# Spreading SSD decay sums and norm factors over the partitions by DMA through DRAM in place of matmuls

## The chip, the cores and the metric

The kernel runs on one core of one Trainium2 chip. The metric is the device time of one execution in microseconds; before the change it is 1229.57 us, the median of three runs (1229.18 to 1230.66). A core has five engines, each with its own queue of instructions that it takes strictly in order: TensorE (PE; its weight loads are listed as PEld), VectorE (DVE), ScalarE (ACT), GpSimd (POOL) and SyncE (SP, which here only issues DMAs). They meet through semaphores. DMA transfers are issued from an engine's queue and carried out by the core's 16 DMA engines.

## The reference, cut to what matters

The program is one layer of a hybrid model on 512 tokens of 1024 values: a norm and an input projection, a state-space branch (SSD), a windowed attention branch, a merge, and a mixture of 64 experts. The change touches two places of the SSD branch: the decay matrix, which needs the running sum `a_cum` of each head along the tokens as rows and as columns, and the group norm at its end.

```
a_cum = jnp.cumsum(dt_c * a.reshape(G, J), axis=2)
seg = a_cum[:, :, :, None] - a_cum[:, :, None, :]
decay = jnp.exp(jnp.where(causal, seg, -jnp.inf)).astype(xs.dtype)
cb = jnp.einsum('bclgn,bcsgn->bclsg', cm, bm)
y_diag = jnp.einsum('bclsgj,bcsgjp->bclgjp', cb[..., None] * decay, xdt)
...
y_off = jnp.einsum('bclgn,bcgjpn->bclgjp', cm, prev) * jnp.exp(a_cum)[..., None].astype(xs.dtype)
y = (y_diag + y_off + xs * d_skip.reshape(G, J)[:, :, None].astype(xs.dtype)).reshape(b, s, SSD_D_INNER)
yz = (y * jax.nn.silu(z)).reshape(b, s, G, SSD_D_INNER // G)
return rms_norm(yz, ssd_norm_g.reshape(G, -1)).reshape(b, s, SSD_D_INNER)
```

There are 32 heads in 4 groups, and 4 chunks of 128 tokens. `rms_norm` takes one factor for each token and group.

## The kernel before

**Stages.** The work goes in two parts. The first, up to about 745 us, makes the projections, the two branches and the merge. Nearly all of its matmuls are projections: `proj` loads 1 MB of weights into one of two buffers `w`, splits each half into a high and a low part (`split`: ScalarE line 181, VectorE or GpSimd line 182, four buffers `g`) and multiplies 512 columns three times per 128 rows (lines 196 to 198). The second part streams 192 expert matrices of 1 MB through a ring of 14 buffers (`ra`, `rb`, line 779) and multiplies them (lines 904 and 925).

**What sets the order.** The code is written stage by stage (`xbc_stage`, `ssd_main`, `z_stage`, `ssd_norm`, `gate_stage`, the attention stages), and the framework's scheduler interleaves the stages on each engine at build time by its own estimate. After that each engine's order is fixed, and an instruction whose inputs are late holds up all that stands behind it on its engine. This holds for SyncE's queue too, which issues all weight loads.

**The decay sums.** `dt_stage` forms `acum` (128 tokens of a chunk on the partitions, 4 chunks times 32 heads as columns), transposes it, and keeps it as a high and a low half in `aT`, heads on the partitions. For each of the 32 heads, `decay` in `ssd_main` spreads the head's row of 512 sums over all 128 partitions by one matmul with a column of `sel` (line 365, into a PSUM tile `sb`). From it ScalarE takes an exponential (line 368, tile `E`), VectorE a minimum with the column sums (line 369, tile `M`), ScalarE four exponentials in place (line 374), VectorE or GpSimd a product with `cbm` (line 386), and PE multiplies (lines 382 and 390 in `heads`). `heads` ends with lines 392 and 394 on VectorE, which empty the two PSUM tiles `y`.

**The norm.** `ssd_norm` runs once for each of the four groups. PE sums the squares (line 406), VectorE scales (line 408), GpSimd takes the power -0.5 (line 409). The factors then lie on the partitions, by token, and are wanted along the columns: VectorE puts them on a diagonal (line 412, four instructions), PE multiplies by ones (line 414), and VectorE applies them from PSUM (line 418, four instructions). Lines 420 and 421 split the result for the next projection.

Small tiles of all these steps come from a pool `v` of 10 buffers of 512 columns, given out in turn.

Of the kernel before, what the change touches and what calls it, by code (L numbers as in the profile page):

```python
# [7 lines left out]
F = mybir.dt.float32  # L8
R = mybir.dt.float32r
# [3 lines left out]
AF = mybir.ActivationFunctionType  # L13
OP = mybir.AluOpType
# [16 lines left out]
def tile_hybrid(ctx: ExitStack, tc: tile.TileContext, x, pos, cols, rows, g2d, wrd, wdtd, wcm, wqkv, wso, wao, wo,  # L31
                wgu, wdn, out):
    nc = tc.nc
    V, S, T, G = nc.vector, nc.scalar, nc.tensor, nc.gpsimd
# [4 lines left out]
    def ptile(tag, bufs=2, dt=F):  # L39
        return psum.tile([128, 512], dt, name=tag, tag=tag, bufs=bufs)  # L40
# [26 lines left out]
    V.memset(half, 0.5)  # L67
    sel = pb.tile([128, 32], R, name="sel")
    G.memset(sel.bitcast(F), 0.0)
    V.tensor_tensor(sel[0:64], ident[0:64, 0:32], ident[0:64, 32:64], op=OP.add)  # L70
    colt = pb.tile([128, 168], F, name="colt")
# [45 lines left out]
    gwd = dram.tile([1024, 1], F, name="gwd")  # L117
    gtd = dram.tile([2, 8, 128, 512], F, name="gtd")

    def wslot(pool, tag, bufs, dt=F):  # L120
# [18 lines left out]
    def g_(): return tk(pg, "g", 4, 1024, R)  # L139
    def v_(dt=F, n=512): return pv.tile([128, n], dt, name="v", tag="v", bufs=10, padded_shape=[128, 512])  # L140
    def c_(dt=F, n=512): return pc.tile([128, n], dt, name="c", tag="c", bufs=6, padded_shape=[128, 512])
# [64 lines left out]
    nacum = pb.tile([128, 128], F, name="nacum")  # L206
    aT = pb.tile([128, 512], R, name="aT")
    G.memset(aT[64:128].bitcast(F), 0.0)

    def dt_stage():  # L210
# [6 lines left out]
        p = ptile("mm")  # L217
# [44 lines left out]
        S.activation(dec, dec, AF.Exp)  # L262
        a2 = v_(n=256)
        a2v = a2.rearrange("p (t u h) -> p t u h", t=4, u=2)
        for u in range(2):
            V.tensor_copy(a2v[:, :, u, :], acum.rearrange("p (t h) -> p t h", t=4))
        pt = ptile("tp")
        for t in range(4):
            T.transpose(pt[0:64, t * 128:(t + 1) * 128], a2[:, t * 64:(t + 1) * 64], ident)
        S.activation(aT[0:32], pt[0:32], AF.Copy)  # L270
        hv = v_(R)
        S.activation(hv[32:64], pt[32:64], AF.Copy)
        V.tensor_tensor(aT[32:64], pt[32:64], hv[32:64].bitcast(F), op=OP.subtract)

# [47 lines left out]
    def ssd_main(g):  # L322
# [37 lines left out]
        def decay(i, u):  # L360
            h = 8 * g + 2 * i + u
            if u == 0:
                Es[i] = v_()
            pb_ = ptile("sb")
            T.matmul(pb_, sel[:, h:h + 1].to_broadcast([128, 128]), aT, start=True, stop=True)
            M = v_()
            us = slice(u * 64, (u + 1) * 64)
            S.activation(Es[i][us, 0:384], pb_[us, 128:512], AF.Exp)
            V.tensor_tensor(M.rearrange("p (c l) -> p c l", c=4), pb_.rearrange("p (c l) -> p c l", c=4),
                            acum.rearrange("p (c h) -> p c h", c=4)[:, :, h:h + 1].to_broadcast([128, 4, 128]),  # L370
                            op=OP.min)
            for c in range(4):
                s = slice(c * 128, (c + 1) * 128)
                S.activation(M[:, s], M[:, s], AF.Exp, bias=nacum[:, c * 32 + h:c * 32 + h + 1])
            return M

# [26 lines left out]
    def ssd_norm(g):  # L403
# [5 lines left out]
        G.tensor_tensor(rs, rs, mhalf.to_broadcast([128, 4]), op=OP.pow)  # L409
        dg = v_()  # L410
        for t in range(4):
            V.tensor_scalar(dg[:, t * 128:(t + 1) * 128], ident, rs[:, t:t + 1], None, op0=OP.mult)
        pr = ptile("sb")
        T.matmul(pr, ones, dg, start=True, stop=True)
        for i in range(4):
# [871 lines left out]
```

## Time and profile before

| | |
|---|---|
| median of three runs | 1229.57 us |
| the profiled execution | 1228.64 us |
| its span in the trace | 1226.8 us |
| PE busy | 1136.3 us, 93% |
| VectorE busy | 656.5 us, 54% |
| ScalarE busy | 388.6 us, 32% |
| GpSimd busy | 239.3 us, 20% |
| bytes moved by DMA | 273.86 MB |

The span is the part of the execution between the first and the last instruction of the trace; the remaining 1.8 us lie around it. Engine times are sums of instruction durations. PE's instructions overlap (the next begins before the last has ended), so what one PE instruction costs is read from the distance between starts, not from its duration. Idle time of an engine that nobody waits for costs nothing.

### The profile page before, as it was taken

Reading aid. Unit: us, or ns where it says so; the run is one execution under the profiler, and the core shown is the slowest. Engines: PE = TensorE matmul, PEld = TensorE weight load, DVE = VectorE, ACT = ScalarE, POOL = GpSimd, SP = SyncE. Lnnn points to the kernel's source line nnn. Section 1 sums busy time; section 2 is a strip of 40 time slices with the busy share of each in tenths; the row PEclk is TensorE's granted clock in tenths of the full one; section 3 lists DMA queues with packets and bytes.
Section 4 is the critical chain, followed back from the end, with each engine's and each line's share of the span. In section 5 each row is a group of like instructions: output and inputs, shape, how many; then the busy total and the mean of one; then the engine's idle time right before and its main releaser. Section 6 shows DMA issues by size and latency. Waiting matters only on the chain.

```text
span 1226.8 us, 16583 instructions
## 1 busy us (share of the span) xinstructions
PE 1136.3 (93%) x6552; PEld 772.2 (63%) x6552; DVE 656.5 (54%) x1224; ACT 388.6 (32%) x796; POOL 239.3 (20%) x195
## 2 busy tenths in 40 slices
PE   6999999999999999999999959999897899999885
PEld 5777778877878988988778956443342434434321
DVE  5958584569536678877665464634422233331422
ACT  5456453464326455634432311110110011111000
POOL 3033431143024533330120241001001001000100
PEclk9999999999999999999999989999999899999999
DMA  4231213221221222222357257999999999999995
GB/s 157 98 118 38 100 61 129 94 79 54 83 104 35 70 104 87 87 69 69 137 168 300 110 235 305 419 420 420 420 419 421 420 415 398 387 420 419 421 419 221
DMA packets 43120, 273.86 MB, mean 223 GB/s; under 512 B 5024, under 2 KB 5664, under 8 KB 11808
## 3 DMA queue, kind: packets, MB, share of 16 engines
q1 hardware_dynamic: 39744, 263.34, 54.1%
q0 software_dynamic: 1712, 7.34, 1.6%
q10 hardware_dynamic: 1584, 2.10, 0.6%
q8 instruction: 52, 0.85, 0.3%
q14 instruction: 28, 0.23, 0.1%
HBM read 266.47 MB, written 6.29 MB: 222 GB/s over the span
## 4 chain that ended last, share of the span: by engine, by line
PE 77%; DVE 10%; DMA 8%; issue 2%; ACT 2%; POOL 1%; SPq 0%; DVEq 0%; ACTq 0%; POOLq 0%
PE mm L196 11%; PE mm L198 11%; PE mm L197 11%; PE mm L904 11%; PE y L925 5%; PE tp L884 5%; DMA rb<-in_wgu_dram 3%; PE tp L1003 3%; DVE acc L1005 2%; PE mm L481 2%; PE tp L1004 2%; PE mm L480 2%; DMA ra<-in_wdn_dram 2%; DMA rb<-in_wdn_dram 2%; PE mm L482 2%
## 5 line engine op out<-in xcount | busy, mean ns | idle before, releaser
L196 PE MATMUL mm<-h,g 128*128 128x512 f32 x448 | 180.7, 403 | 0.8 <-DVE c L309 0.5
L197 PE MATMUL mm<-h,g 128*128 128x512 f32 x448 | 179.8, 401 | 0.0
L198 PE MATMUL mm<-h,g 128*128 128x512 f32 x448 | 178.5, 399 | 0.8 <-POOL g L182 0.8
L904 PE MATMUL mm<-rb,st 128*32 128x512 f32 x712 | 145.6, 619 | 13.3 <-DMA rb<-in_wgu_dram 13.3
L181 ACT ACTIVATE g<-w 128x1024 fp32r<-128x1024 f32 x100 | 105.6, 1057 | 139.4 <-PE mm L197 99.0
L182 DVE TENSOR_TENSOR g<-w,g 128x1024 fp32r<-128x1024 f32 x78 | 98.7, 1265 | 72.9 <-ACT g L181 69.9
L1005 DVE TENSOR_TENSOR acc<-acc,tp 128x512 f32<-128x512 f32 x132 | 86.1, 684 | 37.2 <-PE tp L1004 37.0
L993 POOL TENSOR_SCALAR wk<-dr,vcol 128x512 fp32r<-128x512 int16 x17 | 26.6, 1565 | 383.8 <-PE tp L1004 347.9
L198 PEld LDWEIGHTS mm<-h,g 128*128 128x128 f32 x448 | 84.4, 188 | 22.2 <-POOL g L182 1.5
L196 PEld LDWEIGHTS mm<-h,g 128*128 128x128 f32 x448 | 84.5, 189 | 20.3 <-issue 1.2
L197 PEld LDWEIGHTS mm<-h,g 128*128 128x128 f32 x448 | 84.5, 189 | 19.8 <-issue 1.7
L182 POOL TENSOR_TENSOR g<-w,g 128x1024 fp32r<-128x1024 f32 x22 | 53.8, 2446 | 169.3 <-ACT g L181 138.5
L904 PEld LDWEIGHTS mm<-rb,st 128*32 128x32 f32 x712 | 30.9, 113 | 79.9 <-issue 55.8
L925 PE MATMUL y<-rb,n 128*32 128x512 f32 x384 | 72.0, 641 | 4.0 <-ACT n L916 3.3
L904 PE MATMUL mm<-ra,st 128*32 128x512 f32 x312 | 75.5, 597 | 0.0
L884 PEld LDWEIGHTS tp<-oh,hx 128*128 128x128 f32 x480 | 60.1, 191 | 23.6 <-issue 14.9
L931 DVE TENSOR_TENSOR yo<-y,yo 128x512 fp32r<-128x512 f32 x34 | 23.5, 691 | 92.3 <-ACT yo L930 92.3
L884 PE MATMUL tp<-oh,hx 128*128 128x256 f32 x480 | 66.7, 289 | 3.9 <-DVE m L956 3.6
L1003 PE MATMUL tp<-yo,wk 128*128 128x512 f32 x132 | 59.2, 465 | 11.1 <-DVE acc L1005 11.0
L1003 PEld LDWEIGHTS tp<-yo,wk 128*128 128x128 f32 x132 | 23.6, 187 | 69.6 <-DVE acc L1005 39.2
L909 ACT ACTIVATE n<-mm,gts 128x256 f32<-128x256 f32 x17 | 8.0, 473 | 180.6 <-PE mm L904 161.7
L910 DVE SCALAR_TENSOR_TENSOR n<-n,mm 128x256 f32<-128x256 f32 x17 | 7.1, 421 | 92.6 <-ACT n L909 92.6
(378 smaller groups left out, 2269.4 us busy)
## 6 DMA issues: line engine op xcount, KB each, us to landing
rb<-in_wgu_dram SPq DMA_DIRECT2D x89, 1024.0 KB, 15.1
rb<-in_wdn_dram SPq DMA_DIRECT2D x48, 1024.0 KB, 17.8
ra<-in_wgu_dram SPq DMA_DIRECT2D x39, 1024.0 KB, 12.5
w<-in_wcm_dram SPq DMA_DIRECT2D x27, 1024.0 KB, 4.9
ra<-in_wdn_dram SPq DMA_DIRECT2D x16, 1024.0 KB, 18.1
w<-in_wso_dram SPq DMA_DIRECT2D x8, 1024.0 KB, 4.9
w<-in_wqkv_dram SPq DMA_DIRECT2D x6, 1024.0 KB, 4.8
gtd<-c POOLq DMA_DIRECT2D x16, 256.0 KB, 2.5
```

Source lines behind the costliest of these rows:

```text
L181: S.activation(hi[:, :n], src, AF.Copy)
L182: (G if nsp[0] < 3 or nsp[0] % POOL_LO == 0 else V).tensor_tensor(lo[:, :n], src, hi[:, :n].bitcast(F), op=OP.subtract)
L196: T.matmul(p, hi[:, s], mh[k], start=(k == 0), stop=False)
L197: T.matmul(p, hi[:, s], ml[k], start=False, stop=False)
L198: T.matmul(p, lo[:, s], mh[k], start=False, stop=(k == 7))
L480: T.matmul(o, hh[k][:, ts], hi[:, s], start=(k == 0), stop=False)
L884: T.matmul(p[:, u * 256:(u + 1) * 256], hx[h][:, t, (k + u) * 128:(k + u + 1) * 128], oh[:, t], start=(h == 0 and t == 0), stop=(h == 1 an ...
L904: T.matmul(pg[e * 32:(e + 1) * 32], sts[u // 2][:, k, c:c + 32], wt[u, k // 4, e][:, (k % 4) * 512:(k % 4 + 1) * 512], start=(k == 0), sto ...
L925: T.matmul(py[n][e * 32:(e + 1) * 32], hT[:, f * 128 + e * 32:f * 128 + e * 32 + 32], wt[u, 2, e][:, ws], start=(f == 0), stop=(f == 1))
L993: G.tensor_scalar(wk, drow[0], vcol[:, b:b + 1], None, op0=OP.is_equal)
L1003: T.matmul(p, wk[:, t * 128:(t + 1) * 128], yhl[n][0], start=True, stop=False)
L1005: V.tensor_tensor(acc[t][:, ns], acc[t][:, ns], p, op=OP.add)
```

## The change

The row sums no longer pass through PE. `dt_stage` transposes `acum` alone, copies the 32 rows to a tile `aT` and writes them to a DRAM tensor `acd` (64 KB); `sel` and the high and low halves are gone. `decay` loads each head's row into all 128 partitions of `M` by one DMA (256 KB) from SyncE's queue, and lines 368 and 369 of before read `M` in SBUF in place of the PSUM tile. `ssd_norm` writes the factors to a DRAM tensor `rsd` (512 numbers of 4 bytes, each to a place of its own) and loads them into all partitions of a tile `pr` (256 KB); the diagonal and its matmul are gone. The pool `v` has 11 buffers.

```diff
-    sel = pb.tile([128, 32], R, name="sel")
-    G.memset(sel.bitcast(F), 0.0)
-    V.tensor_tensor(sel[0:64], ident[0:64, 0:32], ident[0:64, 32:64], op=OP.add)
...
+    acd = dram.tile([32, 512], F, name="acd")
+    rsd = [dram.tile([1, 512], F, name=f"rsd{g}") for g in range(4)]
...
-    def v_(dt=F, n=512): return pv.tile([128, n], dt, name="v", tag="v", bufs=10, padded_shape=[128, 512])
+    def v_(dt=F, n=512): return pv.tile([128, n], dt, name="v", tag="v", bufs=11, padded_shape=[128, 512])
...
         pt = ptile("tp")
         for t in range(4):
-            T.transpose(pt[0:64, t * 128:(t + 1) * 128], a2[:, t * 64:(t + 1) * 64], ident)
+            T.transpose(pt[0:32, t * 128:(t + 1) * 128], acum[:, t * 32:(t + 1) * 32], ident)
+        aT = v_()
         S.activation(aT[0:32], pt[0:32], AF.Copy)
-        hv = v_(R)
-        S.activation(hv[32:64], pt[32:64], AF.Copy)
-        V.tensor_tensor(aT[32:64], pt[32:64], hv[32:64].bitcast(F), op=OP.subtract)
+        nc.sync.dma_start(acd, aT[0:32])
...
-            pb_ = ptile("sb")
-            T.matmul(pb_, sel[:, h:h + 1].to_broadcast([128, 128]), aT, start=True, stop=True)
             M = v_()
+            nc.sync.dma_start(M, acd[h:h + 1].to_broadcast([128, 512]))
             us = slice(u * 64, (u + 1) * 64)
-            S.activation(Es[i][us, 0:384], pb_[us, 128:512], AF.Exp)
-            V.tensor_tensor(M.rearrange("p (c l) -> p c l", c=4), pb_.rearrange("p (c l) -> p c l", c=4),
+            S.activation(Es[i][us, 0:384], M[us, 128:512], AF.Exp)
+            V.tensor_tensor(M.rearrange("p (c l) -> p c l", c=4), M.rearrange("p (c l) -> p c l", c=4),
...
-        dg = v_()
-        for t in range(4):
-            V.tensor_scalar(dg[:, t * 128:(t + 1) * 128], ident, rs[:, t:t + 1], None, op0=OP.mult)
-        pr = ptile("sb")
-        T.matmul(pr, ones, dg, start=True, stop=True)
+        nc.sync.dma_start(rsd[g].rearrange("o (t p) -> p (o t)", p=128), rs)
+        pr = v_()
+        nc.sync.dma_start(pr, rsd[g].to_broadcast([128, 512]))
```

The scheduler has laid the instructions anew. Three places are shown. Line numbers in the new program are 1 to 10 lower (189 is 190 of before, 358 is the new load of `M`, 402 and 404 are the write and the load of the norm factors).

SyncE's queue from its start, first before: after the loads of `x` and of the small weights it holds weight loads alone up to the attention stage.

```order
L149 DMA x<-in_x_dram 128x512 x8
L152 DMA v<-in_wdt_dram 128x256
L190 DMA w<-in_wcm_dram 128x1024 x2
L190 DMA w<-in_wcm_dram 128x2048 x19
L190 DMA w<-in_wso_dram 128x2048
```

Now the same queue, from the fourth whole weight load to the end of the first norm; `acd` is written early, and the rows of the first two groups stand among the weight loads.

```order
L189 DMA w<-in_wcm_dram 128x2048 x4
L266 DMA acd<-v 32x512
L189 DMA w<-in_wcm_dram 128x2048 x3
L358 DMA v<-acd 128x512 x8
L189 DMA w<-in_wcm_dram 128x2048 x3
L358 DMA v<-acd 128x512
L189 DMA w<-in_wcm_dram 128x2048
L358 DMA v<-acd 128x512 x6
L189 DMA w<-in_wcm_dram 128x2048
L358 DMA v<-acd 128x512
L402 DMA rsd_145<-v 128x4x1
L404 DMA v<-rsd_145 128x512
```

The eight rows of a group stand right behind one or two weight loads, and a weight load comes between the first and the second row of the second group. The write and the load of the norm factors follow each other.

SyncE's queue around the third norm, before: loads alone, of the attention weights (line 470) and of the last SSD and gate weights (line 190).

```order
L470 DMA w<-in_wqkv_dram 128x2048 x3
L190 DMA w<-in_wcm_dram 128x2048 x2
L470 DMA w<-in_wqkv_dram 128x2048
L190 DMA w<-in_wcm_dram 128x2048 x2
L470 DMA w<-in_wqkv_dram 128x2048 x2
```

And now, with the rows of the fourth group and the third and fourth norm (`rsd_147`, `rsd_148`):

```order
L460 DMA w<-in_wqkv_dram 128x2048 x2
L358 DMA v<-acd 128x512
L460 DMA w<-in_wqkv_dram 128x2048
L358 DMA v<-acd 128x512 x7
L402 DMA rsd_147<-v 128x4x1
L189 DMA w<-in_wcm_dram 128x2048
L404 DMA v<-rsd_147 128x512
L189 DMA w<-in_wcm_dram 128x2048
```

A weight load stands between the first and the second row of the fourth group, and another between the write of the third norm's factors and their load.

VectorE's queue at the fourth norm, before. Line 551 empties the transposed queries, line 182 is the low part of a weight half, line 421 the split of the normed result.

```order
L626 TENSOR_TENSOR x<-y,x 128x512
L408 TENSOR_SCALAR v<-tp 128x4
L626 TENSOR_TENSOR x<-y,x 128x512
L551 TENSOR_TENSOR x<-tp,x 64x512
L412 TENSOR_SCALAR v<-ident,v 128x128 x4
L551 TENSOR_TENSOR x<-tp,x 64x512
L182 TENSOR_TENSOR g<-w,g 128x1024
L551 TENSOR_TENSOR x<-tp,x 64x512 x2
L418 SCALAR_TENSOR_TENSOR v<-x,colt,sb 128x512 x4
```

And now (400 is 408 of before, 408 is 418, 541 is 551, 181 is 182, 616 is 626):

```order
L616 TENSOR_TENSOR x<-y,x 128x512
L400 TENSOR_SCALAR v<-tp 128x4
L616 TENSOR_TENSOR x<-y,x 128x512
L541 TENSOR_TENSOR x<-tp,x 64x512 x2
L408 SCALAR_TENSOR_TENSOR v<-x,colt,v 128x512 x4
L181 TENSOR_TENSOR g<-w,g 128x1024
L541 TENSOR_TENSOR x<-tp,x 64x512
L411 TENSOR_TENSOR y<-v,y 128x512 x4
```

The four instructions that use the factors have moved up: fewer instructions stand between them and the scaling that starts the norm, and the split of a weight half and two of the four query copies now stand behind them.

## Rows read from the trace of the kernel before

**Rows 1.** Page, section 1: busy time, share, instructions of each engine.
```profile
PE 1136.3 (93%) x6552; PEld 772.2 (63%) x6552; DVE 656.5 (54%) x1224; ACT 388.6 (32%) x796; POOL 239.3 (20%) x195
```

**Rows 2.** Stretches: PE, PEld, DVE, ACT, POOL busy; PEclk; DMA share; GB/s.
```profile
450.00:500.00 50.00, 49.57 (x339) 42.75 (x338) 40.45 (x88) 25.46 (x67) 16.30 (x13) 1.00 0.26 83
800.00:1227.00 427.00, 367.44 (x2087) 151.38 (x2085) 139.44 (x260) 45.73 (x85) 23.57 (x16) 0.96 0.97 401
```

**Rows 3.** PE waits: releaser, us in total, times, longest.
```profile
PE sb L414 <- DVE v L412: 1.5, 1, 1.5
```

**Rows 4.** Timeline, PE: start, us, line, operation, count.
```profile
64.68 0.71 PE L365 MATMUL sb<-aT,sel 128*128 128x512 f32 x2
65.23 0.39 PE L196 MATMUL mm<-h,g 128*128 128x512 f32 x1
```

**Rows 5.** Timeline, PE, fourth norm.
```profile
490.48 1.02 PE L414 MATMUL sb<-v,one 128*128 128x512 f32 x2
491.57 0.39 PE L198 MATMUL mm<-h,g 128*128 128x512 f32 x1
```

**Rows 6.** Groups by line and form: count, busy us, mean ns, idle before.
```profile
L369 DVE TENSOR_TENSOR v<-sb,acum 128x512 f32<-128x512 f32 x32 | 21.2, 683 | 5.3 <-ACT v L368 5.2
L386 DVE TENSOR_TENSOR v<-v 128x512 f32<-128x512 f32 x16 | 12.5, 783 | 2.5 <-ACT v L374 2.3
L374 ACT ACTIVATE v<-v,nacum 128x128 f32<-128x128 f32 x128 | 40.0, 390 | 11.5 <-DVE v L369 11.4
L412 DVE TENSOR_SCALAR v<-ident,v 128x128 f32<-128x128 f32 x16 | 10.5, 719 | 0.3 <-POOL v L409 0.3
L409 POOL TENSOR_TENSOR v<-v,mh 128x4 f32<-128x4 f32 x4 | 4.1, 1030 | 7.3 <-DVE v L408 7.3
```

**Rows 7.** Timeline, VectorE, first norm.
```profile
168.01 0.15 DVE L408 TENSOR_SCALAR v<-tp 128x4 f32<-128x4 f32 x1
...
172.28 1.23 DVE L182 TENSOR_TENSOR g<-w,g 128x1024 fp32r<-128x1024 f32 x1 [0.26 <-ACT g L181]
173.42 0.55 DVE L392 TENSOR_TENSOR v<-y,v 128x384 f32<-128x384 f32 x1
174.00 0.75 DVE L394 SCALAR_TENSOR_TENSOR x<-x,colt,y 128x512 f32<-128x512 f32 x1
175.12 2.72 DVE L418 SCALAR_TENSOR_TENSOR v<-x,colt,sb 128x512 f32<-128x512 f32 x4 [0.37 <-PE sb L414]
```

**Rows 8.** Landing of c<-gtd, L681, issued at 629.28 us.
```profile
DMA to landing us min/median/max: 2.7/2.7/2.7
```

**Rows 9.** Landing of c<-gtd, L681, issued at 632.76 us.
```profile
DMA to landing us min/median/max: 5.7/5.7/5.7
```

**Rows 10.** DMA issues by line: KB each, median us to landing.
```profile
post<-in_pos_dram ACTq DMA_DIRECT2D x1, 2.0 KB, 5.6
```

**Rows 11.** Timeline, ScalarE, third norm.
```profile
393.93 1.06 ACT L181 ACTIVATE g<-w 128x1024 fp32r<-128x1024 f32 x1 [1.55 <-PE mm L481]
```

**Rows 12.** Timeline, VectorE, third norm.
```profile
389.92 0.15 DVE L408 TENSOR_SCALAR v<-tp 128x4 f32<-128x4 f32 x1
```

**Rows 13.** Timeline, VectorE, fourth norm.
```profile
483.94 0.15 DVE L408 TENSOR_SCALAR v<-tp 128x4 f32<-128x4 f32 x1
...
486.63 0.69 DVE L551 TENSOR_TENSOR x<-tp,x 64x512 fp32r<-64x512 f32 x1
...
492.14 2.72 DVE L418 SCALAR_TENSOR_TENSOR v<-x,colt,sb 128x512 f32<-128x512 f32 x4
```

**Rows 14.** Timeline, SyncE queue: two weight loads.
```profile
148.62 0.33 SPq L190 DMA_DIRECT2D w<-in_wcm_dram  x1
...
373.50 0.33 SPq L470 DMA_DIRECT2D w<-in_wqkv_dram  x1
```

**Rows 15.** Timeline, PE: first head products of groups 1 and 3.
```profile
156.34 0.43 PE L390 MATMUL y<-v,x 128*64 128x128 f32 x2
...
379.03 0.43 PE L390 MATMUL y<-v,x 128*64 128x128 f32 x2
```

More of the change, by code (lines that the diff above doesn't have):

```diff
@@ L206, in tile_hybrid @@
     nacum = pb.tile([128, 128], F, name="nacum")
-    aT = pb.tile([128, 512], R, name="aT")
-    G.memset(aT[64:128].bitcast(F), 0.0)
     def dt_stage():
@@ L262, in dt_stage @@
         S.activation(dec, dec, AF.Exp)
[L263 to L266, printed above, removed]
         pt = ptile("tp")
         for t in range(4):
-            T.transpose(pt[0:64, t * 128:(t + 1) * 128], a2[:, t * 64:(t + 1) * 64], ident)
+            T.transpose(pt[0:32, t * 128:(t + 1) * 128], acum[:, t * 32:(t + 1) * 32], ident)
+        aT = v_()
         S.activation(aT[0:32], pt[0:32], AF.Copy)
-        hv = v_(R)
-        S.activation(hv[32:64], pt[32:64], AF.Copy)
-        V.tensor_tensor(aT[32:64], pt[32:64], hv[32:64].bitcast(F), op=OP.subtract)
+        nc.sync.dma_start(acd, aT[0:32])
     dt_stage()
```

## Prediction

> **What bounds the kernel now.** I read the engines' busy times first. PE is busy for 93% of the span and no other engine for more than 54% [rows 1]: the reader is to see that PE sets the first part. The stretches come next. Late in that part PE is busy 49.57 of 50 us at a granted clock of 1.00, that is 2.4 GHz, and VectorE, at 40.45 of 50, is the next to fill up; from 800 us on the DMA share is 0.97 [rows 2]. So in the first part a microsecond of PE work or of PE waiting counts in full, and the last part, whose stream of weights is limited by DMA, starts earlier or later by the same amount and keeps its length. DMA has room in the first part (share 0.26), so the 9.4 MB that the change adds (36 loads of 256 KB) cost no bandwidth; what they can cost is latency. Then PE's own waits: the new code removes one of them, 1.5 us for the diagonal [rows 3].
>
> **What is removed.** In the row of two spreading matmuls the next instruction starts 0.55 us after the first, so one takes 0.275 us of PE (its listed duration is longer, since it overlaps the next); 32 of them are 8.8 us [rows 4]. The norm's matmul is listed as two. From the first of them to the start of the projection after the next it is 1.09 us, which holds one projection matmul; taking 0.28 for that, 0.81 us remains, and four norms give 3.2 us [rows 5]. With the wait of 1.5 us, 13.5 us leave PE's path. VectorE loses the 16 diagonal instructions, 10.5 us of its time [rows 6]; I count no gain for this beyond the 1.5 us, since in the trace PE waited for them only once. The smaller tiles of the decay stage (`sel`, the second half of `aT`, some 2 us of VectorE and GpSimd before 62 us) lie beside projections and count nothing; were this cover gone they would give back at most as much. The eleventh buffer pays for the new tile `pr` and for the longer life of `M`, which is now filled early; I cost it at nothing.
>
> **What the norm gains in latency.** In its place comes a chain: scale (0.15 us) and power (1.03 us) as before [rows 6, 7], then a write to DRAM, then a load. The engine that waits is VectorE, at the four instructions that apply the factors, and what is queued behind them is what PE takes next: emptied `y` tiles at the first norm, the low part of a weight half at the fourth. The load is the same kind of transfer as the merge's gate loads, 256 KB onto 128 partitions: 2.7 us when alone [rows 8], 5.7 us when issued 0.6 us behind a weight load [rows 9]. The write is not in the trace: 2 KB in 512 pieces. It could be as quick as a plain transfer alone, 2.7 us [rows 8]. The row nearest to it is the other transfer of 2 KB in small pieces, the positions, 5.6 us, although that one shared the start with other loads [rows 10]. I take 5.6 by the nearest row and keep 2.7 as the low end.
>
> The four places, with the times of before as the clock and the new order of VectorE:
> - First norm: scaling at 168.01, power done at 169.2, write landed at 174.8, load at 177.5. Between stand only lines 392 (0.55), 386 (0.78), 369 (0.68), 182 (1.23) and 394 (0.75), 4.0 us in all [rows 6, 7], done at 172.1. VectorE is idle for 5.4 us; in the kernel before it waited 0.37.
> - Second norm: the chain is 0.15 + 1.03 + 5.6 + 2.7 = 9.5 us, and the new order has ten instructions between: a split of 1.2 us and nine others, for which I take 0.7 us each from the rows of the first norm, 7.5 us. Idle 2.0 us.
> - Third norm: a weight load stands between write and load, and it waits for the split that empties its buffer. ScalarE starts the first part of that split at 393.93 [rows 11], so line 182 is done at 395.0 + 1.2 = 396.2, the load of the factors is issued at about 396.6 and lands 5.7 us later, at 402.3. The scaling is at 389.92 [rows 12]; after the split VectorE has lines 369, 392, 386 and 394, 2.8 us, to 399.0. Idle 3.3 us.
> - Fourth norm: scaling at 483.94, power done at 485.1, write landed at 490.7, load at 493.4. Between stand one copy and two query copies, the second of which ended at 487.3 [rows 13]. Idle 6.1 us. Before, four copies and a split stood there and the factors were applied at 492.14 without a wait.
>
> Together 16.8 us. How much of VectorE's idle time PE feels, the trace can't say: nothing (PE has other projections queued) to all of it. I take all, because the engine is 80% busy there [rows 2] and the inputs of PE's next work stand behind. With a write of 2.7 us the four are 2.5, 0, 3.3 and 3.2, together 9.0 us.
>
> **What the decay rows gain in latency.** A row's DMA can be issued long ahead where its buffer is free, but SyncE takes its queue in order, and the weight loads ahead of it wait for a buffer. Where the first two rows of a group stand behind different loads, the second decides. In group 1 it stands behind the load of 148.62, in group 3 behind that of 373.50 [rows 14]: issued 0.33 us later, landed 5.7 us after that (154.7 and 379.5), then the minimum (0.68), four exponentials (40.0 us for 128, so 0.31 each) and the product (0.78) [rows 6]: 157.4 and 382.2. The first head products began at 156.34 and 379.03 [rows 15]: late by 1.0 and 3.2 us, together 4.2. In groups 0 and 2 all rows stand behind a load some 10 us ahead of the first product, and the sum has nothing for them. The low end is 0 (projections cover it), the high end 8.4, if the later heads of a group are late by as much again. The other way round, the weight loads now stand behind rows that wait for a free `M`; they had 10 us and more to spare, and I cost that at nothing; without the spare time each would be a late split.
>
> **Two inputs in SBUF.** Line 369 read PSUM and now reads `M` in SBUF. With one input in PSUM it takes 683 ns, while line 386, same size with both in SBUF, takes 783 ns in the mean [rows 6]: 32 times 0.1 is 3.2 us of VectorE. I take half of it as reaching PE, 1.6 us, with 0 and 3.2 as ends. The Trainium skill ("SBUF — State Buffer", section "SBUF: two separate sides") says that a VectorE instruction with two SBUF inputs and a GpSimd instruction that reads SBUF exclude each other, the later one blocking fully; the difference of the two rows agrees, and by the rule the loss could be larger wherever the two meet.
>
> **Sum.** -13.5 + 16.8 + 4.2 + 1.6 = +9.1 us. The profiled execution took 1228.64 us, so 1237.7; it lies 0.93 us under the median of the runs, so the forecast is 1238.5 us.
>
> **Rivals.**
> - The two sides cancel: the write lands like a plain transfer, in 2.7 us. Then the sum is -13.5 + 9.0 + 4.2 + 1.6 = +1.3, so 1231 us. For it speaks that 2 KB are little and the DMA engines are three quarters idle; against it the positions' row. The Trainium skill ("DMA: Bandwidth & Descriptors", section "Anatomy of one DMA — SWDGE (gpsimd) path") gives a fixed part of about 2.0 us plus bytes over the rate; by that, for the GpSimd path, the write would be an estimated 2.0 us and the sum about -1. The same page's section "Specifications" speaks the other way: pieces under 512 B are done as read-modify-write. No run here shows either yet.
> - PE is fed all the same, and the kernel gets faster. Mechanism: the low parts of weights are made a half tile ahead (four buffers `g`), so VectorE's idle time never reaches PE. For it: VectorE lost 10.5 us to the diagonal and PE waited once, 1.5 us. Against it: the new order puts the split behind the factors at the fourth norm. Then only part of the matmul saving is lost to the late rows of group 3: -13.5 + 3.2 = -10.3, so 1219 us. It decides as long as VectorE's idle time at each place stays under the projections that PE has queued between the norm's sums and the next use.
> - Every transfer of the norm falls behind a weight load: write and load 5.7 us and more. With 3 us more for the load at the first, second and fourth place, 3 more for the write there, and the high end for the rows, the sum is 9.1 + 18 + 4.2 = +31, so 1261 us. For it: SyncE's order has a weight load close ahead of each of these writes. Against it: most of these loads are issued some microseconds earlier and will have landed.
>
> **How the numbers follow.** A difference under 0.2% (2.5 us) can't be told from none. Chances: forecast 55%, cancelling 18%, faster 14%, all behind loads 13%. The forecast spreads over +3 to +18; its lowest edge gives 2% to the same. Cancelling gives 11% to the same, 4% to slower, 3% to faster; the faster case 12% to faster, 2% to the same. So faster 15%, same 15%, slower 70%. The range reaches from 1226 to 1252 us: it leaves out the greater part of the faster case and most of the heaviest.
>
> **What would show it.** Right: VectorE waits for the DMA of `pr` at the four norms, longest at the fourth, with PE then waiting for line 182's successor or for a `y` tile; ScalarE or VectorE waits for `M` at the start of groups 1 and 3; PE's spreading matmuls gone and its clock still 1.00. Wrong: no VectorE wait for `pr` of over 2 us, or such waits without PE waits after them (then faster); a write of the factors that lands within 3 us (then cancelling); PE waiting chiefly for weight loads (then a cover that I called free is not).

## The result, and the profile after

The changed kernel takes 1268.88 us (median of four runs, 1268.12 to 1270.31) against 1229.38 us for the kernel before (1227.46 to 1230.66): a ratio of 1.0325, with a 95% interval of 1.0312 to 1.0338. It is slower by 39.5 us. The forecast was slower by 9 us, with a range that ended at 1252 us. The profiled execution took 1268.3 us, its span is 1266.5 us. Line numbers of the changed kernel are one to ten lower than before: 400 and 401 are the scaling and the power (408, 409 before), 402 and 404 the write and the load of the factors, 408 applies them (418), 361 is the minimum (369), 181 the low part (182).

The page's busy times, to set beside [rows 1]:

```profile
PE 1139.2 (90%) x6512; PEld 776.7 (61%) x6512; DVE 651.4 (51%) x1204; ACT 390.2 (31%) x797; POOL 244.9 (19%) x193
```

40 matmul records fewer, and yet PE is busy 2.9 us longer. Where the time went is read from one start: the first matmul of the stage behind the merge (line 737 before, 727 after) starts at 663.4 us before and at 700.5 us after. So 37.1 us of the loss lie in the first part, and the last part, 563.4 us long before, takes 566.0 us. The first part of each kernel (columns as in [rows 2]), before and after:

```profile
0.00:663.40 663.40, 647.91 (x3577) 529.21 (x3578) 445.78 (x783) 313.06 (x645) 189.59 (x158) 1.00 0.28 96
0.00:700.50 700.50, 649.00 (x3536) 532.09 (x3537) 440.69 (x763) 314.59 (x645) 195.10 (x156) 0.97 0.32 106
```

PE stands idle for 51.5 us of it in place of 15.5. Its busy time stays (+1.1 us), although the sum took some 12 us of matmuls out; the granted clock is 0.97 in place of 1.00.

VectorE's waits (releaser, us in total, times, longest), the one for the factors, which was 0.37 us at the first norm before [rows 7]:

```profile
DVE v L408 <- DMA v<-rsd: 42.4, 4, 12.2
```

The landing of the four DMA kinds that the change adds (tile, queue, count, KB each, median us), to set beside [rows 8 to 10]:

```profile
v<-acd SPq DMA_DIRECT2D x32, 256.0 KB, 6.3
v<-rsd SPq DMA_DIRECT2D x4, 256.0 KB, 4.2
acd<-v SPq DMA_DIRECT2D x1, 64.0 KB, 1.6
rsd<-v SPq DMA_DIRECT2D x4, 2.0 KB, 10.3
```

The smallest transfer is the slowest: 2 KB in 512 pieces of 4 bytes take 10.3 us (8.3 to 10.8), while 64 KB of the row sums take 1.6. Each load of the factors waits in SyncE's queue for the write before it, 39.2 us at the four norms together, and the weight loads stand behind it. VectorE at the fourth norm, to set beside [rows 13]:

```profile
509.53 0.15 DVE L400 TENSOR_SCALAR v<-tp 128x4 f32<-128x4 f32 x1
...
524.80 2.74 DVE L408 SCALAR_TENSOR_TENSOR v<-x,colt,v 128x512 f32<-128x512 f32 x4 [12.17 <-DMA v<-rsd]
```

From the scaling to the factors 15.3 us pass (8.2 before), and VectorE stands 12.17 of them. What PE then waits for (same columns as the waits above):

```profile
PE mm L471 <- DVE g L181: 11.2, 3, 8.6
...
PE mm L470 <- ACT g L180: 9.6, 1, 9.6
...
PE y L374 <- DVE v L384: 7.9, 2, 7.3
PE mm L195 <- DVE c L302: 7.0, 1, 7.0
```

One long stall for each norm: 7.3, 7.0, 9.6 and 8.6 us, 32.5 together, and none of this kind before. The third comes by way of ScalarE: its copy of the normed result (line 410) waits 14.5 us for VectorE's line 408, and the high parts of the weights (line 180) stand behind it in its queue. The stalls are followed by a second loss. PE around the fourth stall (start, us):

```profile
519.82 0.28 PE L470 MATMUL mm<-g,h 128*128 128x256 f32 x1
528.73 0.58 PE L471 MATMUL mm<-g,h 128*128 128x256 f32 x1 [8.63 <-DVE g L181]
529.11 0.41 PE L472 MATMUL mm<-g,h 128*128 128x256 f32 x1
529.32 0.41 PE L470 MATMUL mm<-g,h 128*128 128x256 f32 x1
...
535.79 0.28 PE L471 MATMUL mm<-g,h 128*128 128x256 f32 x1
535.91 0.28 PE L472 MATMUL mm<-g,h 128*128 128x256 f32 x1
```

Behind the stall the same matmuls start 0.21 us apart, later 0.12. The stretches from the end of each stall to about full speed (columns as in [rows 2]):

```profile
183.60:190.00 6.40, 6.40 (x20) 5.37 (x21) 5.89 (x9) 2.68 (x5) 1.47 (x2) 0.57 0.31 86
...
300.60:306.00 5.40, 5.40 (x14) 4.29 (x15) 4.19 (x7) 1.58 (x3) 4.86 (x2) 0.57 0.01 3
...
432.40:439.00 6.60, 6.51 (x33) 6.51 (x34) 3.63 (x11) 0.00 (x0) 3.73 (x3) 0.55 0.46 159
...
528.70:535.00 6.30, 6.00 (x29) 5.80 (x29) 6.20 (x7) 1.64 (x3) 2.88 (x2) 0.59 0.37 96
```

The granted clock, 1.00 (2.4 GHz) in the first part before, is 0.55 to 0.59 here: most of each stretch ran at 1.2 GHz, after 7 to 10 us in which PE stood. Width times what is missing to 1.00 gives 2.8, 2.3, 3.0 and 2.6 us, 10.7 together: an estimate of the most that it can have cost.

### The profile page after: what moved, and what is told of

The parts are those of the page before. It is cut to its first block, busy times and chain, and to the rows that moved or that the text cites. A ratio compares the mean times of both kernels' runs of the same rounds, so it can differ in the third digit from the quotient of the medians.

```text
span 1266.5 us, 16578 instructions
## 1 busy us (share of the span) xinstructions
PE 1139.2 (90%) x6512; PEld 776.7 (61%) x6512; DVE 651.4 (51%) x1204; ACT 390.2 (31%) x797; POOL 244.9 (19%) x193
## 4 chain that ended last, share of the span: by engine, by line
PE 70%; DMA 14%; DVE 9%; ACT 3%; issue 2%; POOL 1%; SPq 0%; DVEq 0%; POOLq 0%; ACTq 0%
PE mm L894 10%; PE mm L195 10%; PE mm L197 10%; PE mm L196 10%; PE y L915 5%; DMA rb<-in_wgu_dram 5%; PE tp L874 5%; DMA rsd<-v 3%; PE tp L993 3%; DVE acc L995 2%; DMA v<-acd 2%; PE tp L994 2%; DMA ra<-in_wdn_dram 2%; DMA v<-rsd 1%; PE mm L471 1%
## 5 line engine op out<-in xcount | busy, mean ns | idle before, releaser
L195 PEld LDWEIGHTS mm<-h,g 128*128 128x128 f32 x448 | 85.7, 191 | 29.0 <-DVE c L302 7.6
L197 PEld LDWEIGHTS mm<-h,g 128*128 128x128 f32 x448 | 85.6, 191 | 21.8 <-POOL g L181 1.2
L196 PEld LDWEIGHTS mm<-h,g 128*128 128x128 f32 x448 | 85.6, 191 | 18.8 <-issue 0.5
L915 PE MATMUL y<-rb,n 128*32 128x512 f32 x384 | 76.6, 667 | 3.4 <-ACT n L906 3.3
L921 DVE TENSOR_TENSOR yo<-y,yo 128x512 fp32r<-128x512 f32 x34 | 23.5, 691 | 96.5 <-ACT yo L920 96.5
L471 PE MATMUL mm<-g,h 128*128 128x256 f32 x192 | 57.2, 299 | 11.3 <-DVE g L181 11.2
L470 PE MATMUL mm<-g,h 128*128 128x256 f32 x192 | 56.4, 297 | 9.6 <-ACT g L180 9.6
```

The costliest lines, as they stand in the source:

```text
L195: T.matmul(p, hi[:, s], mh[k], start=(k == 0), stop=False)
L196: T.matmul(p, hi[:, s], ml[k], start=False, stop=False)
L197: T.matmul(p, lo[:, s], mh[k], start=False, stop=(k == 7))
L470: T.matmul(o, hh[k][:, ts], hi[:, s], start=(k == 0), stop=False)
L471: T.matmul(o, hh[k][:, ts], lo[:, s], start=False, stop=False)
L915: T.matmul(py[n][e * 32:(e + 1) * 32], hT[:, f * 128 + e * 32:f * 128 + e * 32 + 32], wt[u, 2, e][:, ws], start=(f == 0), stop=(f == 1))
```

## The experiments

All are set against the kernel before on the same chip. "First part" is the start of the matmul named above, "wait" VectorE's wait for the factors, both from the profiled execution (that of norm_16b took 1250.6 us, 6 us over its median).

| kernel | median us | ratio (95% interval) | first part | wait |
|---|---|---|---|---|
| before | 1229.4 | 1 | 663.4 | - |
| after | 1268.9 | 1.0325 (1.0312 to 1.0338) | 700.5 | 42.4 |
| rows_only | 1231.3 | 1.0006 (0.9991 to 1.0022) | 665.2 | - |
| norm_only | 1267.7 | 1.0311 (1.0290 to 1.0332) | 701.6 | 38.8 |
| norm_wide | 1243.0 | 1.0098 (1.0069 to 1.0127) | 671.7 | 7.0 |
| norm_16b | 1244.8 | 1.0115 (1.0099 to 1.0131) | 679.1 | 8.8 |
| norm_only_wide | 1236.5 | 1.0052 (1.0034 to 1.0070) | 667.7 | 5.0 |
| norm_only_16b | 1247.4 | 1.0133 (1.0114 to 1.0152) | 676.4 | 10.4 |
| write_twice | 1296.3 | 1.0538 (1.0517 to 1.0559) | 724.0 | 69.2 |
| norm_late | 1250.8 | 1.0165 (1.0128 to 1.0203) | 681.3 | none |
| filler | 1275.0 | 1.0355 (1.0336 to 1.0375) | 708.2 | 40.6 |
| filler_norm | 1274.3 | 1.0355 (1.0336 to 1.0374) | 708.4 | 42.6 |
| rows_psum | 1236.2 | 1.0062 (1.0041 to 1.0083) | 666.7 | - |
| rows_split15 | 1231.7 | 1.0013 (1.0001 to 1.0024) | 660.9 | - |

**Which half of the change.** Each half alone: in rows_only the norm keeps the diagonal and its matmul, in norm_only the decay sums keep their matmuls.

```diff
 rows_only: ssd_norm as before, cut to two lines
+            V.tensor_scalar(dg[:, t * 128:(t + 1) * 128], ident, rs[:, t:t + 1], None, op0=OP.mult)
+        T.matmul(pr, ones, dg, start=True, stop=True)
 norm_only: decay as before, cut to one line
+            T.matmul(pb_, sel[:, h:h + 1].to_broadcast([128, 128]), aT, start=True, stop=True)
```

> The decay rows by DMA, the norm by diagonal and matmul as before. Theory A (the loss is the norm's write in 4-byte pieces and the waits behind it): the rows alone save PE's 8.8 us and give back little, so 1219 to 1229 us, likeliest 1223. Theory B (the loss is the decay rows: their loads stand among the weight loads in SyncE's queue and wait for buffers of v): 1250 us or more.

> The norm by DMA, the decay sums by matmul as before. Theory A: the loss is all here, and without the 8.8 us that the rows save: 1262 to 1280 us, VectorE waiting some 40 us for pr at the four norms. Theory B: 1225 to 1240 us.

The norm carries all of it: 38.7 us slower alone, while the rows change nothing (0.06%, the interval holds zero). That is less than theory A gave the rows, which were to win some 6 us: rows_only missed its range, 1219 to 1229. Theory B falls. The two halves add up to the whole.

**Is it the write's form?** The write made of 4 pieces of 512 bytes (turned on VectorE), and of 128 pieces of 16 bytes (read back with a stride), in the changed kernel and with the norm's half alone:

```diff
 norm_wide, norm_only_wide (rw holds the factors in 32 columns; the loop over b is left out)
+            V.transpose(rw[0:32, 32 + b * 32:64 + b * 32], rw[b * 32:(b + 1) * 32, 0:32])
+        nc.sync.dma_start(rsd[g].rearrange("o (t p) -> (o t) p", p=128), rw[0:4, 32:160])
 norm_16b, norm_only_16b
-        nc.sync.dma_start(rsd[g].rearrange("o (t p) -> p (o t)", p=128), rs)
+        nc.sync.dma_start(rsd[g].rearrange("o (p t) -> p (o t)", p=128), rs)
-            V.scalar_tensor_tensor(yn, xsT[ch], sng[:, ch:ch + 1], pr, ...)
+            V.scalar_tensor_tensor(yn..., xsT[ch]..., sng[:, ch:ch + 1], pr.rearrange("x (p t) -> x t p", t=4), ...)
```

> The changed kernel, but the factors are turned on VectorE (four 32x32 transposes for each norm) so that the write is 4 pieces of 512 bytes in place of 512 of 4 bytes. Theory A: the write lands in 2 to 3 us in place of 10, VectorE's waits fall from 42 us to 5 to 15, PE's stalls at the norms mostly go, the granted clock is back at 0.98: 1222 to 1240 us, likeliest 1230. Theory C (any round trip through DRAM at this place costs this, by its load and by SyncE's queue, whatever the pieces): 1255 us or more.

> The changed kernel with one thing altered: the factors are written by token, the four of a partition side by side (128 pieces of 16 bytes in place of 512 of 4), and VectorE reads them back with a stride of four. Same instructions in the same order. If the 4-byte pieces are the loss: the write lands in about 2.6 us in place of 10.3, VectorE's wait for pr falls from 42.4 us to 8 to 15, PE's stalls of 7 to 10 us at the norms and the falls of the clock behind them go, and the time is 1232 to 1242 us. If any trip through DRAM at this place costs it: over 1255 us.

> The same alteration with the decay sums by matmul as before. If the 4-byte pieces are the loss, 1228 to 1238 us in place of 1267.7; else over 1255 us.

> The norm by DMA with the write in 4 pieces of 512 bytes (turned on VectorE, which adds 3 to 4 us of its time over four norms), read back contiguously, the decay sums by matmul as before. If the adjacent 4-byte pieces were the loss: the round trip takes some 4.5 us, VectorE waits 5 to 10 us in all and the time is 1229 to 1238 us. If a trip through DRAM costs PE beyond VectorE's waits: over 1240 us.

Of norm_16b first the landing of its write and load, then VectorE's wait:

```profile
v<-rsd SPq DMA_DIRECT2D x4, 256.0 KB, 4.0
rsd<-v SPq DMA_DIRECT2D x4, 2.0 KB, 1.4
```

```profile
DVE v L408 <- DMA v<-rsd: 8.8, 4, 3.6
```

Same bytes and the same instructions; around the norms SyncE's order is the same, and VectorE's but for one step of the convolution (line 304), which stands behind the second norm's factors and no longer ahead of them. The write lands in 1.4 us in place of 10.3, the wait falls from 42.4 to 8.8 us and the time by 24.1 us, of 39.5. With the norm's half alone the 512-byte form takes back 32 of 38.7 us (norm_only_wide is 1.0052 of before, norm_only 1.0311). The form of the write is thus shown to be the main cause, and theory C falls. Only norm_only_wide lies in its expected range, the other three came out 3 to 9 us above theirs. For the two with the stride a reason stands in the groups of the applying instruction (ns min/median/max), first of norm_16b, then of the changed kernel:

```profile
L408 DVE SCALAR_TENSOR_TENSOR v<-x,colt,v x16: 1135/1160/2001, 177.2 to 504.8; 128x512 f32<-128x512 f32 x16
```

```profile
L408 DVE SCALAR_TENSOR_TENSOR v<-x,colt,v x16: 739/747/753, 181.6 to 526.8; 128x512 f32<-128x512 f32 x16
```

0.41 us each, 6.6 us for 16, on the engine that PE waits for. In norm_wide and norm_16b PE also has a stall of 3.3 and 3.7 us at 112 us that the rows bring (below). The cleanest price of a norm by DMA with a quick write is therefore norm_only_wide: 0.52% slower, still no gain over the diagonal.

**What makes the write slow.** Three kernels like the one before, with one unused write of the factors at each norm, in other forms:

```diff
 write_forms, one of them at each of the four norms
+            nc.sync.dma_start(wxa, rs)
+            nc.sync.dma_start(wxb.rearrange("(t p) q -> p t q", p=128), rb_.rearrange("p (t q) -> p t q", t=4))
+            nc.sync.dma_start(wxc, rs[:, 0:1])
+            nc.sync.dma_start(wxd.rearrange("o (t p) -> p (o t)", p=128), rs)
```

> The kernel before with one unused write of the factors to DRAM at each norm, nobody waits for them: 128 pieces of 16 bytes at the first, 512 of 128 bytes at the second, 128 of 4 bytes at the third, 512 of 4 bytes at the fourth. If the number of pieces sets the landing: 2 to 4, about 10, 2 to 4, about 10 us. If their being under 512 bytes or lying on 128 partitions sets it: all four about 10 us. The kernel's time as before within 0.3%, unless the small pieces hold up the weights: then over 1235 us.

> The kernel before with one unused write at each norm: 512 pieces of 16 bytes at the first, 256 of 8 bytes at the second, 512 of 4 bytes each 512 bytes apart in DRAM at the third, 512 of 4 bytes each 64 bytes apart at the fourth. If only pieces as small as 4 bytes are slow: about 2, 2 to 3, 10, 10 us. If it is 4-byte pieces that lie side by side in DRAM: about 2, 4 to 7, 2 to 3, 3 to 5 us. If many small pieces are slow whatever their size: the first near 8 to 10.

> The kernel before with one unused write at each norm, the forms at other places than in the two runs before: 512 pieces of 4 bytes side by side at the first, 512 of 4 bytes 64 bytes apart at the second, 512 of 4 bytes 16 bytes apart at the third, 128 of 4 bytes side by side at the fourth. If lying side by side sets the landing: about 10, 2, between 2 and 6, about 7 us. If the place in the kernel (what else DMA moves then) set it: the first near 2.6 and the fourth near 10.

The landings, each line one write; first write_forms, where wxb is 512 pieces of 128 bytes, wxa 128 of 16, wxc 128 of 4, wxd 512 of 4 bytes:

```profile
wxb<-v SPq DMA_DIRECT2D x1, 64.0 KB, 1.8
wxa<-v SPq DMA_DIRECT2D x1, 2.0 KB, 2.6
wxc<-v SPq DMA_DIRECT2D x1, 0.5 KB, 7.0
wxd<-v SPq DMA_DIRECT2D x1, 2.0 KB, 10.1
```

Then write_forms2: 512 of 16 bytes (wxa), 256 of 8 (wxb), 512 of 4 bytes 512 bytes apart (wxc) and 64 bytes apart (wxd):

```profile
wxa<-v SPq DMA_DIRECT2D x1, 8.0 KB, 2.6
wxb<-v SPq DMA_DIRECT2D x1, 2.0 KB, 2.9
wxc<-v SPq DMA_DIRECT2D x1, 2.0 KB, 1.9
wxd<-v SPq DMA_DIRECT2D x1, 2.0 KB, 1.9
```

And write_forms3: 512 of 4 bytes side by side (wxa, first norm), 64 bytes apart (wxb), 16 bytes apart (wxc), 128 side by side (wxd, fourth norm):

```profile
wxa<-v SPq DMA_DIRECT2D x1, 2.0 KB, 9.0
wxb<-v SPq DMA_DIRECT2D x1, 2.0 KB, 2.0
wxc<-v SPq DMA_DIRECT2D x1, 2.0 KB, 2.6
wxd<-v SPq DMA_DIRECT2D x1, 0.5 KB, 7.0
```

Neither the number of pieces (512 land in 1.8 to 2.6 us in five forms) nor their size alone (512 of 4 bytes land in 1.9 to 2.6 us when they lie apart) is slow. What is slow is 4-byte pieces side by side in DRAM: 7.0 us for 128, 8.3 to 10.8 for 512, at the first norm as at the fourth. Most of the other forms were seen once or twice, and why 4-byte neighbours are slow no run tells. In the first of the three runs neither of my two readings was right as it stood. The unused writes cost next to nothing (write_forms 1.0013, 1.0004 to 1.0023; write_forms2 and write_forms3 ran once, 1230.8 and 1228.3 us).

**What the slow write does to other transfers.** Those issued while it is under way land late too. First the changed kernel: a weight load issued 0.46 us behind the third write, and a store of the gate issued 2.5 us behind the first; then the same weight load in norm_16b:

```profile
w<-in_wcm_dram SPq DMA_DIRECT2D x1, 1024.0 KB, 14.6
gtd<-c POOLq DMA_DIRECT2D x1, 256.0 KB, 9.4
w<-in_wcm_dram SPq DMA_DIRECT2D x1, 1024.0 KB, 6.2
```

The median of these weight loads is 5.0 us in the changed kernel, that of the gate stores 2.7. From 60 us to the merge no engine's wait is put down to a load of `w` there, and write_forms, where a gate store beside the fourth write took 6.6 us, is only 0.13% slower; that the delay costs time of its own is not shown.

**Does the latency reach PE one to one?** The write done twice, one after the other:

```diff
+        for _ in range(2):
             nc.sync.dma_start(rsd[g].rearrange("o (t p) -> p (o t)", p=128), rs)
```

> The changed kernel with the norm's write done twice, the second after the first, and the load after both: some 10 us more of latency at each of the four norms. If the latency of the write reaches PE through VectorE one to one, 40 us more and some further fall of the clock: 1305 to 1318 us. If PE has other work in front of it by then, or the loss is the number of things in SyncE's queue, under 1285 us.

```profile
DVE v L409 <- DMA v<-rsd: 69.2, 4, 18.3
```

The second writes land in about as long as the first, but VectorE's wait grows by 26.8 us and not by 40; its order was laid anew, and at the first norm, for one, line 384 now stands ahead of the factors. The first part grows by 23.5 us and the time by 27.5: nearly one to one with the wait, and between the two ranges that I gave, since I had the wait too large.

**Taking VectorE out of the way.** The same slow write, but the four applying instructions tied to a later tile and called later (the calls are left out here):

```diff
+        V.scalar_tensor_tensor(sl, late[g][:, 0:4], 0.0, sng[:, 4 * g:4 * g + 4], op0=OP.mult, op1=OP.add)
-            V.scalar_tensor_tensor(yn, xsT[ch], sng[:, ch:ch + 1], pr, op0=OP.mult, op1=OP.mult)
+            V.scalar_tensor_tensor(yn, xsT[ch], sl[:, i:i + 1], pr, op0=OP.mult, op1=OP.mult)
```

> The changed kernel, with the same write, but the four instructions that apply the factors are tied by a small multiply-add (128x4, zero times a later tile) to a point two to four projection halves later, so that VectorE does not stand at them. Theory A: the write still takes 10 us, nobody waits for it, and the 13.5 us that PE saves are left: 1214 to 1228 us. Theory C or a theory by which the many small pieces slow other transfers: 1245 us or more. If the x tiles that are held longer hold up the convolutions, between the two.

VectorE has no wait for the factors left, and 18 of the 39.5 us are won back, not all. At 1250.8 us it is a miss for theory A and lies where I put theory C and the slowing of other transfers. PE's waits show what came in their place:

```profile
PE mm L195 <- DVE a L436: 5.0, 2, 3.4
...
PE tp L340 <- DVE v L324: 3.3, 1, 3.3
PE tp L543 <- DVE c L504: 3.2, 1, 3.2
PE mm L196 <- DVE y L418: 2.1, 1, 2.1
```

PE waits for VectorE at other places. At the waits for L504 and L418 the applying instructions (2.7 us in one piece) and the low parts behind them (L418) stand ahead; the two for L436 come behind a wait of VectorE for GpSimd, and the one at L340 is the rows' stall at 112 us (below). Behind these short stalls the granted clock falls too (0.83 from 100 to 120 us, 0.85 from 440 to 460). From 60 us to the merge no wait is put down to a load of `w`, so the slowing of other transfers is not seen to cost this, but norm_late does not rule it out.

**The clock.** Matmuls that nobody reads, to keep PE at work in the stalls:

```diff
 filler: in qkv_tile
+            for _ in range({0: 34, 3: 30}.get(ct, 0) if tp == 0 else 0):
+                T.matmul(p, hh[0][:, 0:128], hh[0], start=True, stop=True)
 filler_norm: before xbc_stage(3) and q_stage(0), 7 and 9 of
+            T.matmul(p, ones, rss[g][:, 0:1].to_broadcast([128, 512]), start=True, stop=True)
```

> The changed kernel with matmuls whose result nobody reads (128x512, two inputs that lie ready) set just before the query-tile matmuls at which PE stood 9.6 and 8.6 us after the third and fourth norm: 34 and 30 of them, some 7 to 8 us of PE each, less than the stalls. If the fall of the granted clock in those stalls is part of the loss (after them matmuls started 0.214 us apart in place of 0.12 for 5 us, 2.3 us lost each), PE stays at 1.00, the stretches after the stalls run at full speed and the time falls by 3 to 5 us, to 1264 to 1266. If only the waits count, it stays at 1268 to 1270; if the fillers come late and are in the way, it rises.

> The changed kernel with matmuls whose result nobody reads, 7 just ahead of PE's stall at the second norm (7.2 us) and 7 just ahead of that at the third (9.8 us), 2 more somewhat earlier; they read the factors as soon as GpSimd has them, and take by the norm's matmul of before some 0.8 us each, 5.6 us at each place, less than the stall. If the clock's fall is a loss of its own, the stalls shrink to 1 to 4 us, the stretches behind them run at a granted clock nearer 1.00 and the time falls by 2 to 4 us, to 1265 to 1267. If it costs nothing, 1268 to 1270. If the added matmuls hold up what VectorE waits for, over 1271 us.

Neither gained: in time, both landed where I had put added matmuls that are in the way. In filler the PSUM tile that the added matmuls write came free only at the end of the third stall (PE waited 7.4 us for it), so they were added to the stall. In filler_norm they ran ahead of the second stall, of which about 3.5 us remained, and the clock fell all the same. At the third, stalls of 3.0 and 2.9 us remained, and the clock from 435.4 to 442 us was 0.56. Around the second:

```profile
300.00:306.00 6.00, 2.52 (x18) 1.77 (x18) 6.00 (x10) 2.52 (x4) 1.38 (x1) 0.76 0.01 3
306.00:312.00 6.00, 6.00 (x23) 4.59 (x20) 2.37 (x4) 2.06 (x3) 4.24 (x3) 0.67 0.00 0
```

Some of the 5 to 6 us by which both lie above the changed kernel are a stall of PE ahead of 112 us (3.4 and 3.2 us, next paragraph), which the profiled execution of the changed kernel does not have. What the clock costs apart from the waits is so read from the distances of the matmuls and from the sum over the first part alone; no run isolates it.

**Where the rows' gain went.** 32 matmuls of 0.275 us [rows 4] are gone from rows_only, and it is no faster. PE has one new stall there; below it the stretch that follows, columns as in [rows 2]:

```profile
112.64 0.47 PE L337 MATMUL tp<-ident,x 128*128 128x128 f32 x1 [3.19 <-DVE v L321]
```

```profile
112.64:119.00 6.36, 6.18 (x14) 4.64 (x15) 5.60 (x8) 1.90 (x5) 2.63 (x2) 0.50 0.01 3
```

After only 3.2 us in which PE stood, the granted clock is 0.50 (1.2 GHz) for 6.4 us: up to 3.2 us more by the same estimate. Stall and clock together are an estimated 6.4 of the 8.8 us.

VectorE (first) and GpSimd (second) ahead of it, in the same execution:

```profile
109.16 2.83 DVE L360 TENSOR_TENSOR v<-v,acum 128x512 f32<-128x512 f32 x1
111.91 0.68 DVE L321 TENSOR_TENSOR v<-tp,tri 128x512 f32<-128x512 f32 x1
```

```profile
108.64 2.80 POOL L180 TENSOR_TENSOR g<-w,g 128x1024 fp32r<-128x1024 f32 x1
```

The minimum, 0.68 us before [rows 6], takes 2.83 us beside GpSimd's 2.80. Two runs test it: rows_psum lets the minimum read PSUM again, rows_split15 gives that one piece of GpSimd's work to VectorE.

```diff
 rows_psum
+            S.activation(pb_, M, AF.Copy)
...
 rows_split15
+        (G if nsp[0] < 3 or nsp[0] % POOL_LO == 0 and nsp[0] != 15 else V).tensor_tensor(lo[:, :n], src, ...)
```

> Rows by DMA, norm by matmul as in the run before of that kind, and ScalarE copies each row tile into a PSUM tile, from which the exponential and the minimum read as in the kernel before. It adds 32 ScalarE copies of some 0.5 us (16 us on an engine that is busy a third of the time). If the rows' loss is VectorE's minimum with both inputs in SBUF (28 to 30 us for 32 in place of 21, single ones stretched to 2.8 us beside GpSimd), the minimum is back at 0.68 us, PE's stall of 3.2 us at 112 us goes and the 8.8 us of matmuls are left as a gain: 1219 to 1226 us. If the rows' loss is the latency of their loads or SyncE's queue, it stays at 1229 to 1236 us.

> Rows by DMA, norm by matmul, and the one low part of a weight half that GpSimd makes at 108.6 us, beside the minimum that took 2.83 us, is made by VectorE (1.2 us of it). If PE's stall of 3.2 us at 112 us comes from GpSimd and VectorE holding each other up over SBUF, it goes, the clock stays at 1.00 there, and the time is 1222 to 1228 us. If the rows' loads cause it, it stays at 1230 to 1234 us.

In both the stall at 112 us is gone, so the two engines do hold each other up there; in rows_psum the minimum is back at 0.681 us in the mean, and none of the 32 takes more than 0.693. Neither kernel gets faster for it: by the times alone rows_split15 lies where I put the rival, the loads' latency (1230 to 1234 us), and rows_psum just above its range. rows_psum has 18.6 us of copies on ScalarE and new small stalls (2.5 us for VectorE ahead of 296 us, with a granted clock of 0.58 for 4 us behind it). rows_split15, whose clock stays at 1.00 from 60 us to the merge, ends the first part 2.5 us earlier than the kernel before, but its last part takes 568.4 us in place of 563.4. Why the last part varies by up to 7 us between these kernels (563.4 to 570.8, one execution each, where the runs of rows_only alone lie 8 us apart) no run here tells, so what the rows are worth stays open between -2.5 us at the end of the first part and +2 us at the end.

## Why the prediction was wrong

**The direction and the chain were right.** VectorE waits for the factors at all four norms, longest at the fourth (12.17 us, 12.07 at the third), and PE then waits for the low part of a weight half or a `y` tile, at the third norm for a high part from ScalarE. As the sum assumed, most of VectorE's idle time reaches PE: of 42.4 us, 32.5 in the four long stalls, and write_twice adds 23.5 us to the first part for 26.8 of wait. The rival by which PE is fed all the same falls, and so does the one in which the two sides cancel.

**The mis-sized term is the norm's, +16.8 us, through its write.** I took 5.6 us from the transfer of the same size, the positions [rows 10], and it measured 10.3. With the idle times of 5.4, 2.0, 3.3 and 6.1 us beside the measured 9.82, 8.36, 12.07 (the lines of the first three norms follow) and 12.17 us, the four places are short by 25.6 us; the write's 4.7 us, four times, are 19 of them.

```profile
181.62 1.41 DVE L408 SCALAR_TENSOR_TENSOR v<-x,colt,v 128x512 f32<-128x512 f32 x2 [9.82 <-DMA v<-rsd]
296.71 2.74 DVE L408 SCALAR_TENSOR_TENSOR v<-x,colt,v 128x512 f32<-128x512 f32 x4 [8.36 <-DMA v<-rsd]
424.62 2.74 DVE L408 SCALAR_TENSOR_TENSOR v<-x,colt,v 128x512 f32<-128x512 f32 x4 [12.07 <-DMA v<-rsd]
```

The loads, 3.6, 4.8, 5.1 and 3.1 us in place of 2.7, 2.7, 5.7 and 2.7, are 2.8 more, and what else stood in the queues is the rest. At the third norm the load waited for the write and not, as I had it, for a split that empties a weight buffer. The fault in the working: the row was near in bytes and not in form. The positions are a load, of 16 bytes for each partition. And the range had a low end for the write (2.7) and no high end: 5.6 was taken as the value and as the end at once, for a number that counts four times.

The Trainium skill ("DMA: Bandwidth & Descriptors", section "Specifications"), cited in the forecast against the short estimate, has pieces under 512 bytes done as read-modify-write. The runs show more than that rule tells: pieces of 128, 16 and 8 bytes landed in 1.4 to 2.9 us, like a plain transfer, and only 4-byte pieces that lie side by side took 7 to 11.

**A term that was missing: the clock.** "Its clock still 1.00" was what I expected to see. It fell after each of the four stalls, up to 10.7 us together by the granted clock of the stretches, and the sum put this at nothing without a reason.

**The heaviest rival named the size, not the cause.** +31 us came from weight loads ahead of every transfer of the norm. norm_16b leaves SyncE's order around the norms as it was, the factors' load still lands in 4.0 us there (4.2 in the changed kernel), and the time falls by 24.1 us. That this rival's size came near the measured 39.5 us is luck.

**The matmuls.** -13.5 us was taken for 32 spreading matmuls, the norm's and its wait. norm_only_wide, whose waits for the factors are down to 5.0 us, is still 0.52% slower than before, so the norm's matmul saves less than even a quick replacement costs. In rows_only PE's busy time before the merge is 3.0 us less, and not 8.8. **The decay rows' latency** (+4.2) and **the two inputs in SBUF** (+1.6) were both to be small: together with -8.8 they gave -3.0, and the half alone measured +0.06%, within the bounds of 0 to 8.4 and 0 to 3.2. ScalarE does wait for the rows at the start of the second and the fourth group, as forecast, 1.05 and 4.43 us in the changed kernel, but no wait of PE over 1 us follows. The minimum's cost was misjudged in kind: 32 of them take 28.0 us in the changed kernel in place of 21.2 [rows 6], most at 0.685 and single ones up to 1.78 us (2.83 in rows_only), where a mean of 0.1 us more was assumed. The Trainium skill ("SBUF — State Buffer", section "SBUF: two separate sides"), by which the later of the two engines blocks fully, fits the 2.83 us beside 2.80 in rows_only.

**A sum of the forecast that does not come out.** With a write of 2.0 us the four idle times are 1.8, 0, 3.3 and 2.5 us, so that variant of the cancelling rival gives -0.1 us and not about -1. Nothing else hangs on it.

## What to carry to other kernels

Size an unseen transfer by the nearest row in form (direction, piece size, whether the pieces are neighbours in DRAM), not in bytes, and give the value that counts four times a high end too. A small value that must cross partitions through DRAM should be written in pieces of 8 bytes or more, or apart, and other transfers behind a slow write should be looked at too. Even a quick round trip (1.4 and 4.0 us in norm_16b) in front of an in-order engine that feeds TensorE cost more here than the matmul that it replaced; scheduling past the slow one (norm_late) won back 18 us and not all. Where an added wait stops TensorE, look at the granted clock behind it before summing only the wait: here it fell behind a stall of 3.2 us too.

## What was not expected of the hardware

- 512 pieces of 4 bytes side by side in DRAM land in 8.3 to 10.8 us, 128 of them in 7.0; the same 512 pieces 16, 64 or 512 bytes apart in 2.6, 1.9 to 2.0 and 1.9 us.
- A 1 MB weight load issued 0.46 us behind such a write landed in 14.6 us, where the median is 5.0.
- A VectorE instruction that reads one 128x512 input with a stride of 16 bytes took 1.16 us in place of 0.75.
- TensorE's granted clock fell to 1.2 GHz after stalls of 7 to 10 us, in filler_norm also where only about 3.5 us of the stall remained, and after single stalls of 3.2 us (rows_only) and 2.5 us (rows_psum). In the changed kernel matmuls of 256 columns then started 0.21 us apart in place of 0.12 for some 5 us.
